# Forms of two pairs of inner channels made in one place, and a second new pass of each round begun by sums, in a gated-attention and MLP layer on one core

## The chip, the cores and the metric

The kernel runs on one core of one Trainium2 chip, launched once. The metric is the time on the device in microseconds; times given are the median of repeated runs. A profile is one more execution, recorded by the hardware profiler; its times count from the start of its span.

## What is computed

One layer (`DEPTH` is 1, so only the first mixer is used): RMSNorm, chunk-causal gated linear attention and its output projection, added to the residual; RMSNorm and an MLP with squared ReLU, added again; a last RMSNorm. 256 tokens, model width 2048, MLP width 8192, all in float32.

```python
def _sq_relu_mlp(h, w_up, w_down):
    a = jax.nn.relu(h @ w_up)
    return (a * a) @ w_down
...
    h = h + _gla_mixer(_rmsnorm(h, gla_norm[j]), ...)
    h = h + _sq_relu_mlp(_rmsnorm(h, mlp_norm[i]), mlp_w_up[i], mlp_w_down[i])
    return _rmsnorm(h, final_norm)
```

The change concerns the MLP. `w_up` is 2048 x 8192 and `w_down` 8192 x 2048.

## The kernel before

**Number format.** TensorE (PE) multiplies 128x128 stationary tiles by 256 moving columns. To keep float32 accuracy each operand is split in two parts, hi and lo: ScalarE (ACT) makes hi by a cast (L118) and VectorE (DVE) makes lo = raw - hi (L131, L154, L964). A product is three matmuls: hi by hi, hi by lo, lo by hi.

**Up.** `up()` (L701) works through 16 groups of 512 inner channels; each takes 8 up steps (L732), one for every two blocks of 128 rows of `w_up`, 24 matmuls a step, into two PSUM banks. When a group is complete, `ends` (L769) gives four pieces of work, one of which is issued behind each of the next four up steps (`piece`, L705): `normalized` (L785) applies ReLU and the RMSNorm scale on DVE, from PSUM into a tile of the pool tag t512; `forms` (L796) squares on ACT into `work[:, 2]` and makes sums and differences on DVE (L802); `form_parts` (L807) splits these into hi (ACT, L812) and lo (DVE, L813), which become stationary tiles of the down products.

**Down.** `down()` (L867) works in 8 rounds `m` of 1024 inner channels. A round is cut into 4 pairs `kp` of two blocks of 128 channels, and into up to four passes, one for each 512 output columns `g`. `order_of` (L667) runs the passes forwards and backwards in turn, so that the first pass of a round has the columns of the last pass of the round before. That one goes on in the same four PSUM banks; the other three passes are new ("fresh") and begin with copies between PSUM and SBUF on ACT (L828).

For one pair, the activations are a 2x2 block matrix (two halves of the tokens, two blocks of channels) and so is the weight. There are two ways to multiply them:

- by blocks: 8 products, 24 matmuls;
- by sums: 7 products of sums of blocks (the scheme of Strassen in Winograd's variant), 21 matmuls. DVE makes sums of the activations once for each pair (the forms S1 to S4) and sums of the weights for each pair and pass: three additions (L930, into `work[:, 0]` and `work[:, 1]` in turn). These sums are then cast (two casts of 512 columns, L118) and their lo is made (L964). In exchange the cast and lo of the weight itself need only 768 of 1024 columns.

`by_sums` (L671) says which way is taken:

```python
        if m == ROUNDS - 1:
            return (g, kp) in ((0, 2), (0, 3), (1, 2))
        if m == ROUNDS - 2 and g == order_of(m)[-1]:
            return kp == 1
        i = order_of(m).index(g)
        return kp > 0 or i == 1 or m > 0 and i == 0
```

A fresh pass whose first pair is by sums is `quick` (L886): two of its four banks are begun at the end of the pass before (L987) and the others while the first pair is at work (L911, L960).

**Order.** The driver (L1022) takes one up step with each pair of the down stage, 18 up steps ahead (`LEAD`, L681). PE's order is fixed by hand (`in_order`, L691). DVE and ACT are kept in order by `issue_after`: a lo follows the last weight sum, sums follow the lo, the copies of PSUM follow the last cast. What is left open is settled at build time by the framework's scheduler; each engine runs its own list in order. The weight slots `hi` and `lo` have five buffers each (L75), raw weights six (L135).

**Placement.** Up pairs listed in `even` (L718) have the second half of their weights shifted by 16 columns in the slot (L148) and, in the lo products, the halves in reverse order (L758).

**Other users of t512** (three buffers of 512 columns): the gate (L357), squares whose result is not used (L542, L619, L1033), `gate_out` (L558) and the diagonal tiles of `scale2_row` (L649).

Of the kernel before, what the change touches and what calls it, by code (L numbers as in the profile page):

```python
# [39 lines left out]
DV = 512  # L40
# [22 lines left out]
ROUNDS = HID // MR  # L63
# [5 lines left out]
def tile_gla_mlp(ctx, tc, x, xt, cols, w_vg, w_in, w_gate, w_out, w_up, w_down, final_norm, out):  # L69
    nc = tc.nc  # L70
# [5 lines left out]
    tmp = ctx.enter_context(tc.tile_pool(name="tmp", bufs=2))  # L76
# [232 lines left out]
    GR = 64 + RANK  # L309
# [44 lines left out]

    vh = big.tile([P, NT, D], F32R, tag="B", name="vh")
    vl = big.tile([P, NT, D], F32R, tag="B", name="vl")
    gn = tmp.tile([P, NT, GR], F32, tag="t512", name="gn", bufs=3)  # L357

    def put_v(bank, n, t, c0):
        nc.scalar.activation(vh[:, t, c0 : c0 + n], bank[:, :n], AF.Copy, scale=r1[:, t : t + 1])  # L360
# [5 lines left out]
    acc = natural(plain_x, rows(w_vg, 0, WMAX), WMAX, cuts, ahead=input_tile)  # L366
# [92 lines left out]
    for half in range(2):  # L459
        acc = turned(stream_x, w_in, KEYW + half * GT, even=(0,) if half else (2, 3), acc=None if half else [aux_bank(), aux_bank()])  # L460
# [18 lines left out]
    for half in range(2):  # L479
        acc = turned(stream_x, w_in, half * GT, even=())  # L480
# [41 lines left out]
    acc = natural(plain_x, rows(w_in, 3 * KEYW), G, HALF)  # L522
# [8 lines left out]
    def attend(hd, t):  # L531
        o = aux_bank()
        blocks = [(0, 0)] if t == 0 else [(0, P), (1, T)]
        vs = slice(hd * DV, (hd + 1) * DV)
        n = 0
        for src, lo in blocks:
            a_h, a_l = (a[hd][:, lo : lo + P] for a in (ath, atl))
            for s, v in ((a_h, vh), (a_h, vl), (a_l, vh)):
                halves(o, s, v[:, src, vs], n == 0, n == 3 * len(blocks) - 1)
                n += 1  # L540
        ss = st.tile([P, 1], F32, tag="oss", name="oss")
        sq = tmp.tile([P, DV], F32, tag="t512", name="sq", bufs=3)  # L542
        nc.scalar.activation(sq, o, AF.Square, scale=r1k[:, t : t + 1], accum_out=ss)
        nc.vector.tensor_scalar(ss, ss, 1.0 / DV, EPS, op0=ALU.mult, op1=ALU.add)
        rs = st.tile([P, 1], F32, tag="ors", name="ors")
        rsqrt(rs, ss)
        nc.vector.tensor_scalar(on[:, t, vs], o, r1k[:, t : t + 1], rs, op0=ALU.mult, op1=ALU.mult)
# [6 lines left out]
    def gate_out(acc, c0):  # L554
        for c in range(2):
            for t in range(NT):
                lo = c0 + 512 * c
                s = tmp.tile([P, 512], F32, tag="t512", name="sr", bufs=3)  # L558
                nc.scalar.activation(s, acc[t][c], AF.Silu, scale=r1[:, t : t + 1])
                nc.vector.tensor_tensor(on[:, t, lo : lo + 512], on[:, t, lo : lo + 512], s, op=ALU.mult)  # L560

# [14 lines left out]
    acc = natural(row_x, rows(w_in, 4 * KEYW), G, HALF, order=(EVEN[0], 0, EVEN[1], *(kt for kt in range(1, KT) if kt not in EVEN)))  # L576
# [24 lines left out]
    acc = natural(row_x, rows(w_in, 5 * KEYW), G, HALF)  # L601
# [13 lines left out]
    def ssq_h(c0):  # L615
        for t in range(NT):
            for c in range(2):
                lo = c0 + 512 * c
                sq = tmp.tile([P, 512], F32, tag="t512", name="sq", bufs=3)  # L619
                nc.scalar.activation(sq, h[:, t, lo : lo + 512], AF.Square, accum_out=hs[:, t, lo // 512 : lo // 512 + 1])  # L620

    acc = natural(row_o, rows(w_out, 0), G, HALF)
# [8 lines left out]
    acc = natural(row_o, rows(w_out, G), G, HALF)  # L631
# [13 lines left out]
    def scale2_row():  # L645

        b = aux_bank()
        for t in range(NT):
            d = tmp.tile([P, P], F32, tag="t512", name="diag", bufs=3)  # L649
            nc.vector.tensor_scalar(d, ident, r2[:, t : t + 1], None, op0=ALU.mult)  # L650
            nc.tensor.matmul(b[:, t * P : (t + 1) * P], ones, d, start=True, stop=True)
        nc.scalar.copy(r2row, b[:, :T])
# [3 lines left out]

    S3, S1, S2, S4, A12, A11, A22, A21 = range(8)
    KP = MR // P // 2  # L660
    GROUPS = D // GT
    work = mid.tile([P, 3 * G + T], F32, tag="qt", name="work")
    r2row = work[:, 3 * G :]
# [7 lines left out]
    def by_sums(m, g, kp):  # L671

        if m == ROUNDS - 1:
            return (g, kp) in ((0, 2), (0, 3), (1, 2))
        if m == ROUNDS - 2 and g == order_of(m)[-1]:
            return kp == 1
        i = order_of(m).index(g)
        return kp > 0 or i == 1 or m > 0 and i == 0


    LEAD = KT + 2  # L681
# [81 lines left out]
    def on_act(i):  # L763
        newest_form[0] = i.ins

    def on_vector(i):
        newest_form[1] = i.ins

    def ends(m, q, acc, taken):  # L769

        act = big.tile([P, 4 * G + 64], F32R, tag="BC"[q], name="act")[:, OFF:-16]
        acts[m][q] = act = act.rearrange("p (b i f s) -> p b i f s", b=2, i=2, f=8)
        normal = []

        def start():
            normal.extend(normalized(b) for b in acc)
            free.extend(taken)

        make = lambda b: forms(m, 2 * q + b, normal[b])
        split = lambda b: form_parts(m, 2 * q + b, act[:, b])  # L780
        if m == ROUNDS - 1 and q == MR // GT - 1:
            return [lambda: (start(), make(0)), lambda: split(0), lambda: make(1), lambda: split(1)]
        return [start, lambda: make(0), lambda: (split(0), make(1)), lambda: split(1)]

    def normalized(bank):  # L785
        s = tmp.tile([P, 2, T], F32, tag="t512", name="su", bufs=3)
        on_vector(nc.vector.scalar_tensor_tensor(
            s, bank.rearrange("p (i t) -> p i t", i=2), 0.0, r2row.unsqueeze(1).to_broadcast([P, 2, T]),
            op0=ALU.max, op1=ALU.mult,
        ))  # L790
        return s

    form = work[:, 2].rearrange("p (f s) -> p f s", f=8)
    ways_of = lambda m, kp: {by_sums(m, g, kp) for g in range(GROUPS)}

    def forms(m, kp, s):  # L796
        f = form
        on_act(nc.scalar.activation(
            f[:, A12:].rearrange("p (t i) s -> p i t s", t=2), s.rearrange("p i (t s) -> p i t s", t=2), AF.Square
        ))  # L800
        if True in ways_of(m, kp):
            sub = lambda o, x, y: on_vector(nc.vector.tensor_tensor(o, x, y, op=ALU.subtract))  # L802
            sub(f[:, S3 : S1 + 1], f[:, A21:].to_broadcast([P, 2, P]), f[:, A11 : A22 + 1])
            sub(f[:, S2], f[:, A11], f[:, S1])
            sub(f[:, S4], f[:, A12], f[:, S2])

    def form_parts(m, kp, act):  # L807
        ways = ways_of(m, kp)
        some = slice(0 if True in ways else A12, 8 if False in ways else A21)
        x = form[:, some].rearrange("p f s -> p (f s)")  # L810
        oh, ol = (act[:, i, some].rearrange("p f s -> p (f s)") for i in range(2))
        on_act(nc.scalar.copy(oh, x))  # L812
        on_vector(nc.vector.tensor_tensor(ol, x, oh.bitcast(F32), op=ALU.subtract))  # L813

    def stationary(m, kp, f):
        return [acts[m][kp // 2][:, kp % 2, i, f] for i in range(2)]
# [3 lines left out]
    n_sums = [0]  # L820
# [46 lines left out]
    def down(passes):  # L867
# [7 lines left out]
        for n, (m, g) in enumerate(passes):  # L875
# [11 lines left out]
            for kp in range(KP):  # L887
# [35 lines left out]
                block = lambda i, n=1: slice(i * T, (i + n) * T)  # L923
                if by_parts:
                    these = (P16, 0, at(A11), block(1)), (B32, T, at(A12), block(3)), (B32, 0, at(S4), block(2))
                    wk = work[:, n_sums[0] % 2]
                    n_sums[0] += 1
                    u = wk.rearrange("p (f s) -> p f s", f=4)
                    raw = raw.rearrange("p (f s) -> p f s", f=4)
                    add = lambda o, x, y: nc.vector.tensor_tensor(o, x, y, op=ALU.add)  # L930

                    with tc.issue_after(last_lo[0].ins):
                        add(u[:, :2], raw[:, :1].to_broadcast([P, 2, T]), raw[:, 1:3])
                        add(u[:, 2], u[:, 0], raw[:, 2])
                        last_sum[0] = add(u[:, 3], u[:, 2], raw[:, 3]).ins
                else:
                    these = [
                        (k, 0, at(f[i]), block(2 * i, 2))
                        for i in range(2) for k, f in ((B32, (A11, A12)), (BX4, (A21, A22)))
                    ]  # L940
# [89 lines left out]

    def square(t, src):
        n = src.shape[-1]
        sq = tmp.tile([P, 512], F32, tag="t512", name="sqf", bufs=3)  # L1033
# [15 lines left out]

    def last_step(kt, w, t, c):  # L1050
        lo, hi = cuts[t][c]
        a = stationary(ROUNDS - 1, kt // 2, (A11, A21)[t] - kt % 2)
# [94 lines left out]
```

## Time and profile before

| | |
|---|---|
| median of 3 runs | 1056.26 us (1055.80 to 1056.47) |
| profiled execution | 1056.75 us |
| its span in the profile | 1054.7 us |
| granted TensorE clock | 0.999 |
| matmuls | 9136 |
| read from and written to HBM | 206.92 MB and 2.10 MB |

The difference between the profiled execution and its span lies before the first and behind the last recorded instruction. A row of instructions shows line, engine, operation, tiles (written <- read), their size and number; in the view by time it shows the start, the length, and in brackets the idle time of the engine before it with what ended it. Lengths of neighbouring instructions overlap, since the next begins before the last results of one are written; the pace of an engine is read from start to start. In the view of stretches each engine has its busy time and, in brackets, its number of instructions.

### The profile page before, as it was taken

The numbers are of one execution on the slowest core, as the hardware profiler recorded it, in microseconds if no ns is written. First come the engines' busy times: TensorE is split into PE (matmuls) and PEld (weight loads), VectorE is DVE, ScalarE is ACT, GpSimd is POOL, SyncE is SP. The second block draws the span as 40 slices with busy tenths as digits, with TensorE's granted clock in tenths as the row PEclk, the third lists the DMA queues.
The fourth block names the chain that finished last, engine by engine and source line by source line (L and its number), as shares of the span: only waits on it lengthen the run. The fifth ranks groups of instructions, "written<-read, shape, count | busy, mean of one in ns | idle before, by whom it ended". The sixth has DMA issues, their size and how long they took to land.

```text
span 1054.7 us, 22398 instructions
## 1 busy us (share of the span) xinstructions
PE 1045.4 (99%) x9136; PEld 1044.4 (99%) x9136; DVE 844.4 (80%) x1169; ACT 697.5 (66%) x1017; POOL 12.7 (1%) x39
## 2 busy tenths in 40 slices
PE   9999999999999999999999999999999999999997
PEld 8999999999999999999999999999999999999997
DVE  5768645656465566889999999999999999999887
ACT  5785544546455455677678778777777777777685
POOL 0000000010000000000000000000000000000000
PEclk9999999999999999999999999999999999999999
DMA  9857665556656666567566566666666666666673
GB/s 341 314 177 212 192 197 160 160 147 177 197 180 181 186 194 180 158 193 226 172 209 217 193 208 207 199 202 201 216 200 202 220 200 201 202 199 207 213 214 127
DMA packets 94790, 210.46 MB, mean 200 GB/s; under 512 B 6704, under 2 KB 7344, under 8 KB 94560
## 3 DMA queue, kind: packets, MB, share of 16 engines
q1 hardware_dynamic: 94016, 207.38, 63.0%
q10 hardware_dynamic: 672, 1.66, 0.5%
q8 instruction: 71, 1.16, 0.5%
q14 instruction: 31, 0.25, 0.1%
HBM read 206.92 MB, written 2.10 MB: 198 GB/s over the span
## 4 chain that ended last, share of the span: by engine, by line
PE 96%; DMA 2%; issue 0%; ACT 0%; SPq 0%; DVE 0%; POOLq 0%; POOL 0%; DVEq 0%; ACTq 0%
PE up L699 33%; PE acc L699 28%; PE acc L165 25%; PE acc L205 6%; PE aux L205 2%; DMA raw<-in_w_vg 1%; PE aux L165 1%; PE aux L568 1%; DMA zz<-in_xt 1%; PE aux L496 1%; SPq L157 0%; ACT sqf L1034 0%; DVE lo L131 0%; ACT hi L118 0%; PE acc L397 0%
## 5 line engine op out<-in xcount | busy, mean ns | idle before, releaser
L118 ACT CAST hi<-raw 128x1024 fp32r<-128x1024 f32 (+3 forms) x386 | 372.7, 986 | 169.8 <-PE acc L165 106.2
L131 DVE TENSOR_TENSOR lo<-raw,hi 128x1024 fp32r<-128x1024 f32 (+3 forms) x226 | 245.7, 1089 | 117.2 <-ACT hi L118 115.7
L699 PE MATMUL acc<-hi,act 128*128 128x256 f32 x1724 | 247.0, 276 | 0.0
L699 PE MATMUL up<-hl,hi 128*128 128x256 f32 x1024 | 239.4, 276 | 0.0
L699 PE MATMUL up<-hh,hi 128*128 128x256 f32 x1024 | 239.3, 276 | 0.0
L154 DVE TENSOR_TENSOR lo<-raw,hi 128x1024 fp32r<-128x1024 f32 x160 | 194.9, 1220 | 36.8 <-ACT hi L118 34.5
L699 PEld LDWEIGHTS acc<-hi,act 128*128 128x128 f32 x1724 | 219.2, 188 | 0.0
L118 ACT CAST hi<-work 128x512 fp32r<-128x512 f32 x196 | 119.9, 622 | 119.0 <-DVE work L930 108.3
L699 PEld LDWEIGHTS up<-hl,hi 128*128 128x128 f32 x1024 | 192.3, 188 | 0.0
L699 PEld LDWEIGHTS up<-hh,hi 128*128 128x128 f32 x1024 | 192.3, 188 | 0.0
L699 PE MATMUL up<-hh,lo 128*128 128x256 f32 x1024 | 137.4, 276 | 0.0
L699 PE MATMUL acc<-lo,act 128*128 128x256 f32 x862 | 134.1, 276 | 0.0
L964 DVE TENSOR_TENSOR lo<-work,hi 128x1024 fp32r<-128x1024 f32 x98 | 119.5, 1220 | 8.9 <-ACT hi L118 8.9
L699 PEld LDWEIGHTS up<-hh,lo 128*128 128x128 f32 x1024 | 126.0, 188 | 0.0
L699 PEld LDWEIGHTS acc<-lo,act 128*128 128x128 f32 x862 | 114.4, 188 | 0.0
L165 PE MATMUL acc<-hi,xA 128*128 128x256 f32 (+1 forms) x736 | 104.7, 279 | 1.0 <-ACT hi L118 1.0
L165 PEld LDWEIGHTS acc<-hi,xA 128*128 128x128 f32 x736 | 93.7, 188 | 1.7 <-ACT hi L118 1.7
L930 DVE TENSOR_TENSOR work<-work,raw 128x256 f32<-128x256 f32 x196 | 83.1, 424 | 5.1
L930 DVE TENSOR_TENSOR work<-raw 128x512 f32<-128x512 f32 x98 | 67.1, 685 | 0.0
L165 PE MATMUL acc<-lo,xA 128*128 128x256 f32 (+1 forms) x368 | 58.5, 278 | 0.1
L165 PEld LDWEIGHTS acc<-lo,xA 128*128 128x128 f32 x368 | 49.6, 188 | 0.3 <-DVE lo L131 0.3
L205 PE MATMUL acc<-xA,hi 128*128 128x256 f32 x288 | 49.2, 276 | 0.0
(158 smaller groups left out, 1148.4 us busy)
## 6 DMA issues: line engine op xcount, KB each, us to landing
raw<-in_w_up SPq DMA_DIRECT2D x128, 512.0 KB, 4.7
raw<-in_w_down SPq DMA_DIRECT2D x128, 512.0 KB, 4.1
raw<-in_w_in SPq DMA_DIRECT2D x80, 512.0 KB, 3.8
raw<-in_w_out SPq DMA_DIRECT2D x32, 512.0 KB, 3.7
raw<-in_w_vg SPq DMA_DIRECT2D x14, 520.0 KB, 8.6
h<-in_x SPq DMA_DIRECT2D x4, 512.0 KB, 8.9
out<-hf SPq DMA_DIRECT2D x5, 256.0 KB, 2.6
zz<-in_xt SPq DMA_DIRECT2D x3, 384.0 KB, 8.2
```

The costliest lines, as they stand in the source:

```text
L118: last_hi[0] = nc.scalar.copy(to, raw)
L131: last_lo[0] = nc.vector.tensor_tensor(lo[:, s], raw[:, s], hi[:, s].bitcast(F32), op=ALU.subtract)
L154: last_lo[0] = nc.vector.tensor_tensor(to[1], dst, to[0].bitcast(F32), op=ALU.subtract)
L165: nc.tensor.matmul(o[:, m], x, w[:, m], start=first and c == 0, stop=last, skip_group_check=True)
L205: nc.tensor.matmul(o, u[:, i, s], m, start=kt == 0 and n == 0 and j % 2 == 0, stop=kt == KT - 1 and n == 2, skip_group_check=True,)
L496: nc.tensor.matmul(o, kab[:, k[0], c0 + c, k[1] : k[1] + P], q(qt[:, c0 + c]), start=c == 0, stop=c == 1)
L568: nc.tensor.transpose(b[:, o + t * P : o + (t + 1) * P], src[:, t, kt * P : (kt + 1) * P], ident)
L699: newest[0] = nc.tensor.matmul(o, x, w, start=first, stop=last, skip_group_check=True).ins
L930: add = lambda o, x, y: nc.vector.tensor_tensor(o, x, y, op=ALU.add)
L964: last_lo[0] = nc.vector.tensor_tensor(to[1][:, :G], wk, to[0][:, :G].bitcast(F32), op=ALU.subtract)
```

## The change

1. `by_sums` takes the first pair of pass i = 3 by sums, as well as that of i = 1 (in rounds 0 to 5).
2. `forms` works for both pairs of a group at once, in `work[:, 1:]` (2048 columns, where one pair had `work[:, 2]`). `normalized` writes there; one square in place of two, three subtractions twice as wide in place of six. The pieces of a group become: both ReLUs; the forms of both pairs; the split of the first; the split of the second. The last group has three pieces in place of four.
3. The weight sums use `work[:, 0]` and a new tile `spare` (2 x 512 columns) in turn. `spare` takes the room of two of the three t512 buffers; it also serves `gate_out` (three of the four tiles) and the diagonal tiles.
4. The forms are renumbered, so that the block that was second is stored in order of PSUM.

```diff
-    gn = tmp.tile([P, NT, GR], F32, tag="t512", name="gn", bufs=3)
+    gn = tmp.tile([P, NT, GR], F32, tag="t512", name="gn", bufs=1)
+    spare = tmp.tile([P, 2, 512], F32, tag="spare", name="spare", bufs=1)
...
-                s = tmp.tile([P, 512], F32, tag="t512", name="sr", bufs=3)
+                i = 2 * c + t
+                s = tmp.tile([P, 512], F32, tag="t512", name="sr", bufs=1) if i % 3 == 2 else spare[:, i % 3]
...
-            d = tmp.tile([P, P], F32, tag="t512", name="diag", bufs=3)
+            d = spare[:, t, :P]
...
-    S3, S1, S2, S4, A12, A11, A22, A21 = range(8)
+    S1, S3, S2, S4, A12, A22, A11, A21 = range(8)
...
-        return kp > 0 or i == 1 or m > 0 and i == 0
+        return kp > 0 or i in (1, 3) or m > 0 and i == 0
...
+    form = work[:, 1:].rearrange("p b (f s) -> p b f s", f=8)
     def ends(m, q, acc, taken):
-        normal = []
         def start():
-            normal.extend(normalized(b) for b in acc)
+            for b in range(2):
+                normalized(acc[b], form[:, b, A12:])
             free.extend(taken)
-        make = lambda b: forms(m, 2 * q + b, normal[b])
-        split = lambda b: form_parts(m, 2 * q + b, act[:, b])
+        split = lambda b: form_parts(m, 2 * q + b, form[:, b], act[:, b])
         if m == ROUNDS - 1 and q == MR // GT - 1:
-            return [lambda: (start(), make(0)), lambda: split(0), lambda: make(1), lambda: split(1)]
-        return [start, lambda: make(0), lambda: (split(0), make(1)), lambda: split(1)]
+            return [lambda: (start(), forms(m, q)), lambda: split(0), lambda: split(1)]
+        return [start, lambda: forms(m, q), lambda: split(0), lambda: split(1)]
...
-    def forms(m, kp, s):
-        on_act(nc.scalar.activation(
-            f[:, A12:].rearrange("p (t i) s -> p i t s", t=2), s.rearrange("p i (t s) -> p i t s", t=2), AF.Square
-        ))
-        if True in ways_of(m, kp):
-            sub(f[:, S3 : S1 + 1], f[:, A21:].to_broadcast([P, 2, P]), f[:, A11 : A22 + 1])
-            sub(f[:, S2], f[:, A11], f[:, S1])
-            sub(f[:, S4], f[:, A12], f[:, S2])
+    def forms(m, q):
+        on_act(nc.scalar.activation(f[:, :, A12:], f[:, :, A12:], AF.Square))
+        if any(True in ways_of(m, 2 * q + b) for b in range(2)):
+            sub(f[:, :, S1 : S3 + 1], f[:, :, A21:].to_broadcast([P, 2, 2, P]), f[:, :, A22 : A11 + 1])
+            sub(f[:, :, S2], f[:, :, A11], f[:, :, S1])
+            sub(f[:, :, S4], f[:, :, A12], f[:, :, S2])
...
-                    wk = work[:, n_sums[0] % 2]
+                    wk = work[:, 0] if n_sums[0] % 2 else spare.rearrange("p b c -> p (b c)")
```

More of the change, by code (lines that the diff above doesn't have):

```diff
@@ L541, in attend @@
         ss = st.tile([P, 1], F32, tag="oss", name="oss")
-        sq = tmp.tile([P, DV], F32, tag="t512", name="sq", bufs=3)
+        sq = tmp.tile([P, DV], F32, tag="t512", name="sq", bufs=1)
         nc.scalar.activation(sq, o, AF.Square, scale=r1k[:, t : t + 1], accum_out=ss)
@@ L618, in ssq_h @@
                 lo = c0 + 512 * c
-                sq = tmp.tile([P, 512], F32, tag="t512", name="sq", bufs=3)
+                sq = tmp.tile([P, 512], F32, tag="t512", name="sq", bufs=1)
                 nc.scalar.activation(sq, h[:, t, lo : lo + 512], AF.Square, accum_out=hs[:, t, lo // 512 : lo // 512 + 1])
@@ L783, in ends, with normalized @@
-        return [start, lambda: make(0), lambda: (split(0), make(1)), lambda: split(1)]
-    def normalized(bank):
-        s = tmp.tile([P, 2, T], F32, tag="t512", name="su", bufs=3)
+            return [lambda: (start(), forms(m, q)), lambda: split(0), lambda: split(1)]
+        return [start, lambda: forms(m, q), lambda: split(0), lambda: split(1)]
+    def normalized(bank, to):
         on_vector(nc.vector.scalar_tensor_tensor(
-            s, bank.rearrange("p (i t) -> p i t", i=2), 0.0, r2row.unsqueeze(1).to_broadcast([P, 2, T]),
-            op0=ALU.max, op1=ALU.mult,
-        ))
-        return s
@@ L793, in tile_gla_mlp @@
-    form = work[:, 2].rearrange("p (f s) -> p f s", f=8)
+            to.rearrange("p (i t) s -> p i (t s)", i=2), bank.rearrange("p (i t) -> p i t", i=2), 0.0,
+            r2row.unsqueeze(1).to_broadcast([P, 2, T]), op0=ALU.max, op1=ALU.mult,
+        ))
     ways_of = lambda m, kp: {by_sums(m, g, kp) for g in range(GROUPS)}
-    def forms(m, kp, s):
+    def forms(m, q):
         f = form
-        on_act(nc.scalar.activation(
-            f[:, A12:].rearrange("p (t i) s -> p i t s", t=2), s.rearrange("p i (t s) -> p i t s", t=2), AF.Square
-        ))
-        if True in ways_of(m, kp):
+        on_act(nc.scalar.activation(f[:, :, A12:], f[:, :, A12:], AF.Square))
+        if any(True in ways_of(m, 2 * q + b) for b in range(2)):
@@ L802, in forms @@
             sub = lambda o, x, y: on_vector(nc.vector.tensor_tensor(o, x, y, op=ALU.subtract))
-            sub(f[:, S3 : S1 + 1], f[:, A21:].to_broadcast([P, 2, P]), f[:, A11 : A22 + 1])
-            sub(f[:, S2], f[:, A11], f[:, S1])
-            sub(f[:, S4], f[:, A12], f[:, S2])
-    def form_parts(m, kp, act):
+            sub(f[:, :, S1 : S3 + 1], f[:, :, A21:].to_broadcast([P, 2, 2, P]), f[:, :, A22 : A11 + 1])
+            sub(f[:, :, S2], f[:, :, A11], f[:, :, S1])
+            sub(f[:, :, S4], f[:, :, A12], f[:, :, S2])
@@ L808, in form_parts @@
+    def form_parts(m, kp, f, act):
         ways = ways_of(m, kp)
         some = slice(0 if True in ways else A12, 8 if False in ways else A21)
-        x = form[:, some].rearrange("p f s -> p (f s)")
+        x = f[:, some].rearrange("p f s -> p (f s)")
         oh, ol = (act[:, i, some].rearrange("p f s -> p (f s)") for i in range(2))
@@ L1032, in square @@
         n = src.shape[-1]
-        sq = tmp.tile([P, 512], F32, tag="t512", name="sqf", bufs=3)
+        sq = tmp.tile([P, 512], F32, tag="t512", name="sqf", bufs=1)
         nc.scalar.activation(sq[:, :n], src, AF.Square, accum_out=fs[:, t, n_fs[t] : n_fs[t] + 1])
@@ L1051, in last_step @@
         lo, hi = cuts[t][c]
-        a = stationary(ROUNDS - 1, kt // 2, (A11, A21)[t] - kt % 2)
+        a = stationary(ROUNDS - 1, kt // 2, ((A11, A12), (A21, A22))[t][kt % 2])
         for i, (x, y) in enumerate(((0, 0), (0, 1), (1, 0))):
```

## Prediction

> **What bounds the kernel now.** I read the head of the page, then TensorE (PE) by stretches, the chain, and VectorE (DVE) and ScalarE (ACT) instruction by instruction through one round. Numbers in the rows of time are us: start, length, what.
>
> ```profile
> span 1054.7 us, 22398 instructions
> PE 1045.4 (99%) x9136; PEld 1044.4 (99%) x9136; DVE 844.4 (80%) x1169; ACT 697.5 (66%) x1017; POOL 12.7 (1%) x39
> ```
>
> PE never rests, so only matmuls taken away, or waits added, can move the end. The average of 80% for DVE hides the stage that matters. Here is one round of the MLP by stretches (busy time and instructions of PE, PEld, DVE, ACT, POOL):
>
> ```profile
> 672.80:693.40 20.60, 20.60 (x184) 20.60 (x184) 20.50 (x32) 14.56 (x20) 0.00 (x0) 1.00 0.55 173
> 693.40:714.00 20.60, 20.60 (x184) 20.60 (x183) 19.84 (x27) 15.78 (x24) 0.00 (x0) 1.00 0.69 222
> 714.00:734.50 20.50, 20.50 (x184) 20.50 (x183) 19.81 (x29) 17.33 (x26) 0.00 (x0) 1.00 0.61 192
> 734.50:755.10 20.60, 20.60 (x184) 20.60 (x183) 18.35 (x24) 14.92 (x22) 0.00 (x0) 1.00 0.73 233
> ```
>
> DVE is busy 78.5 of 82.3 us: PE binds, with DVE 4.6% behind. I call a pair of inner channels of one down pass, with the up step beside it, a unit; a round has 16, u0 to u15, four to each pass. A unit by sums has 21 + 24 = 45 matmuls, one by blocks (a light unit) 24 + 24 = 48. Today u8 and u12 are light in rounds 1 to 5.
>
> The chain in one round, PE's pieces with their matmuls:
>
> ```profile
> 715.26 1.93 PE acc L699 x17
> 720.36 3.63 PE acc L699 x32
> 741.10 3.63 PE acc L699 x32
> ```
>
> A matmul takes 3.63 / 32 = 0.1134. The x32 pieces are the last 8 of the unit before and the 24 of a light unit, so u8 starts at 721.27 and u12 at 742.0. u7 starts at 715.26 + 8 x 0.1134 = 716.17. A heavy unit is 5.10 us, a light one 5.44, so u13 starts at 747.45; a round is 82.3.
>
> **What the change takes away.** `by_sums` now also holds for the first pair of the last pass (i = 3) in rounds 0 to 5 (round 6 returns earlier, in round 7 nothing changes): six light units u12 become heavy. 6 x 3 = 18 matmuls x 0.1134 = **2.04 us** less on PE. The compiled order of the changed kernel has 9087 matmuls in place of 9105; the DMA queue of SP and the work of POOL are in the same order.
>
> **What it adds to DVE.** A heavy unit, and the light u8 with the start of u9, on DVE:
>
> ```profile
> 703.03 0.96 DVE L131 TENSOR_TENSOR lo<-raw,hi 128x768 fp32r<-128x768 f32 x1 [0.29 <-ACT hi L118]
> 703.90 0.69 DVE L930 TENSOR_TENSOR work<-raw 128x512 f32<-128x512 f32 x1
> 704.62 0.88 DVE L930 TENSOR_TENSOR work<-work,raw 128x256 f32<-128x256 f32 x2
> 705.43 1.22 DVE L154 TENSOR_TENSOR lo<-raw,hi 128x1024 fp32r<-128x1024 f32 x1
> ...
> 707.70 0.95 DVE L131 TENSOR_TENSOR lo<-raw,hi 128x768 fp32r<-128x768 f32 x1
> 718.55 1.22 DVE L131 TENSOR_TENSOR lo<-raw,hi 128x1024 fp32r<-128x1024 f32 x1
> 719.69 0.61 DVE L802 TENSOR_TENSOR work<-work 128x128 f32<-128x128 f32 x2
> 720.22 1.22 DVE L154 TENSOR_TENSOR lo<-raw,hi 128x1024 fp32r<-128x1024 f32 x1
> 721.35 0.95 DVE L131 TENSOR_TENSOR lo<-raw,hi 128x768 fp32r<-128x768 f32 x1
> ```
>
> Instructions overlap, so I count from start to start. The heavy unit takes 707.70 - 703.03 = 4.67. The light one takes (719.69 - 718.55) + (721.35 - 720.22) = 2.27 without the two forms. Each new heavy unit costs DVE 2.4 us.
>
> **What the merged forms give back.** Today each pair has one subtraction 256 wide and two 128 wide; after it one 512 and two 256 wide serve two pairs.
>
> ```profile
> 683.22 0.69 DVE L930 TENSOR_TENSOR work<-raw 128x512 f32<-128x512 f32 x1
> 683.83 0.42 DVE L802 TENSOR_TENSOR work<-work 128x256 f32<-128x256 f32 x1
> 684.16 0.42 DVE L930 TENSOR_TENSOR work<-work,raw 128x256 f32<-128x256 f32 x1
> 684.50 0.29 DVE L802 TENSOR_TENSOR work<-work 128x128 f32<-128x128 f32 x1
> 684.70 0.42 DVE L930 TENSOR_TENSOR work<-work,raw 128x256 f32<-128x256 f32 x1
> ```
>
> Start to start: 512 wide 0.61, 256 wide 0.33, 128 wide 0.20. Before 2 x (0.33 + 0.20 + 0.20) = 1.46, after 0.61 + 0.33 + 0.33 = 1.27: 0.2 saved for each up group of 512 channels, 0.4 a round. The square becomes one instruction 1024 wide; a cast that wide starts 0.95 after its predecessor (rows below), two of 512 take 1.06: 0.1 of ACT.
>
> [...]
>
> Sum for DVE in a round: 78.5 busy, about 0.5 lost between dependent additions (in each unit by sums 704.59 to 704.62, and as much inside the pair), + 2.4 - 0.4 = 81.0. PE: 15 x 5.10 + 5.44 = 82.0. DVE alone still fits, by 1.0 us.
>
> **What ACT takes of that 1.0.** A pass that begins by sums has two accumulator copies each ahead of two of its casts. Pass i = 1 (u4, u5) does so today:
>
> ```profile
> 695.55 0.63 ACT L118 CAST hi<-work 128x512 fp32r<-128x512 f32 x1 [0.22 <-DVE work L930]
> 696.09 0.58 ACT L828 COPY acc<-h 128x512 f32<-128x512 f32 x1
> ...
> 697.12 0.83 ACT L118 CAST hi<-raw 128x768 fp32r<-128x768 f32 x1
> 697.99 0.96 DVE L131 TENSOR_TENSOR lo<-raw,hi 128x768 fp32r<-128x768 f32 x1 [0.19 <-ACT hi L118]
> ```
>
> The cast is done 2.4 after the last addition, DVE would be there after 2.27. So DVE loses 0.28 at u4 (693.05, the row below, to 697.99 is 4.94, not 4.66) and 0.38 at u5 (697.99 to 703.03): 0.66 per pass. This wait is tied to DVE's own additions, not to PE. In the changed kernel u12 and u13 have the same ACT order, so two passes lose 1.32.
>
> A third loss is new. From the square before u8 to the cast of u10, ACT runs almost without a gap; the DVE rows are the additions before that square, an idle stretch and the start of u10:
>
> ```profile
> 716.59 0.63 ACT L798 ACTIVATE work<-su 128x512 f32<-128x512 f32 x1
> 717.12 1.04 ACT L118 CAST hi<-raw 128x1024 fp32r<-128x1024 f32 x1
> 718.07 1.10 ACT L828 COPY acc<-h 128x512 f32<-128x512 f32 x2
> 721.19 0.59 ACT L828 COPY sums<-acc 128x512 f32<-128x512 f32 x1 [0.30 <-PE acc L699]
> 727.61 1.80 ACT L118 CAST hi<-raw 128x768 fp32r<-128x768 f32 x2
> 715.14 0.89 DVE L930 TENSOR_TENSOR work<-work,raw 128x256 f32<-128x256 f32 x2
> 726.79 1.23 DVE L964 TENSOR_TENSOR lo<-work,hi 128x1024 fp32r<-128x1024 f32 x1 [0.48 <-ACT hi L118]
> 728.50 0.96 DVE L131 TENSOR_TENSOR lo<-raw,hi 128x768 fp32r<-128x768 f32 x1
> ```
>
> ACT: from 716.59 to 727.61 are 11.0, less the 0.30 for PE 10.7. In the changed order the first square is 0.42 longer, the second (0.53) is gone, and the cast of the second pair's form (0.84 by start to start), which today stands in u10, comes ahead of u10's cast: 11.45. With one cast of the sums before the square (0.56) and u10's own (0.83), 12.85 from the additions' end. DVE: 728.50 - 716.03 = 12.47, of which 0.48 idle; with the wider forms (0.27 before u8, 0.24 in it) 12.5. DVE loses about 0.4 there. So 1.32 + 0.4 = 1.7 lost against 1.0 spare: **0.7 us a round short**. PE must then wait that much in a round, once the store is used up.
>
> **The store.** How far DVE is ahead:
>
> ```profile
> 693.05 0.95 DVE L131 TENSOR_TENSOR lo<-raw,hi 128x768 fp32r<-128x768 f32 x1
> 713.55 0.95 DVE L131 TENSOR_TENSOR lo<-raw,hi 128x768 fp32r<-128x768 f32 x1
> 741.29 0.95 DVE L131 TENSOR_TENSOR lo<-raw,hi 128x768 fp32r<-128x768 f32 x1
> ```
>
> In u7 the part is ready at 714.50 and wanted after six matmuls, at 716.85: 2.35 ahead. In u13, behind the light u12, 742.24 against 748.13: 5.9. That refill goes. By the same steps u10 starts on DVE 2.9 ahead of PE in round 1 (the copy that waits for PE at 721.19 sets it), u2 of the next round 1.5 ahead, where 0.4 is needed; each later round is 0.7 lower. Three further rounds end in stalls: about 0.5 + 0.75 + 0.75 = 2.0.
>
> A stall costs more than itself. Matmuls in 20 us, at full clock (column PEclk):
>
> ```profile
> 30.00:50.00 20.00, 20.00 (x169) 20.00 (x168) 14.50 (x19) 15.02 (x21) 1.07 (x2) 1.00 0.87 302
> 210.00:230.00 20.00, 20.00 (x179) 20.00 (x178) 11.34 (x16) 8.86 (x15) 2.75 (x5) 1.00 0.48 140
> ```
>
> With two or three in each count that lie across an edge, PE's pace is some 5% slower in the first: 0.2 us a unit. I read it as left behind by a wait, until the shifted pair of `even` (L718, in u4) comes by. From u2 to u4 that is 0.4 in a round, and it gives DVE time, so it largely replaces a later stall. I add 0.4 in all.
>
> **Sum.** -2.04 + 2.0 + 0.4 = +0.4 us on the profiled 1056.75 (span 1054.7 and 2.05 around it), 0.5 above the median of 1056.26: 1056.7 against the median.
>
> Costed at nothing: `normalized` writes the same width elsewhere; squares into one t512 buffer follow each other on ACT alone; `gate_out` keeps three buffers; the sums keep two (work and `spare`); the last group has three pieces for four, where PE has no wait. If a form's subtraction waits for the wider square, 0.4 at most a group, 0.8 a round, falls on DVE.
>
> **Rivals.** (a) *The cover holds*: the copies of u12 are absorbed, DVE keeps 1.0 spare, no stall: 1056.26 - 2.04 = 1054.2. For it: DVE loses as much at u4 and u5 today and PE never waits. Against: no second refill. [...]
> (b) *Slower*: PE waits behind u4, in u5 to u15, and keeps the slow pace until the next u4. It decides once u7 or u8 is under 0.4 ahead. Ten units x 0.2 = 2 us a round, in three rounds 6, with 0.7 for the first stalls: 1056.26 - 2.04 + 6.7 = 1061. Against: my ledger has u2 as the lowest point.
> (c) *It doesn't do what it says*: PE's order shows 18 fewer matmuls; under 1%.
>
> **How the numbers follow.** Forecast, 1055 to 1058.4: 0.50; (a) 0.27; (b) 0.22. A run tells 0.2%, 2.1 us, from no change, so the bounds are 1054.15 and 1058.37. (a) lies on the first: 0.10 of it faster, 0.17 same. (b) is slower, with 0.03 of the forecast. Faster 0.10, same 0.65, slower 0.25. An error of 0.3 us a round in the ledger moves the end by 1.4; the range is 1054.1 to 1060.0.
>
> **What would show it.** Right: 18 matmuls fewer; DVE at 98% and more of rounds 2 to 5; waits of PE for DVE or ACT in u1 to u4 from round 3 on, absent before; DVE idle 0.2 to 0.4 at u12 and u13. Wrong: no wait of PE and rounds of 82.0 us (then (a)); matmuls at 0.118 through most of a round (then (b)); a form waiting for its square.

## The result, and the profile after

| | before | after |
|---|---|---|
| median | 1056.37 us (1055.80 to 1056.60) | 1061.91 us (1061.53 to 1061.93) |
| profiled execution | 1056.75 us | 1061.93 us |
| its span | 1054.7 us | 1060.0 us |
| granted TensorE clock | 0.999 | 0.999 |
| matmuls | 9136 | 9118 |

The ratio is 1.0052 (95% interval 1.0035 to 1.0070): 0.5% or 5.5 us longer, clear of the noise, and above the predicted range (1054.1 to 1060.0). The head of the page after:

```profile
span 1060.0 us, 22328 instructions
PE 1050.6 (99%) x9118; PEld 1048.9 (99%) x9118; DVE 855.6 (81%) x1148; ACT 701.4 (66%) x1013; POOL 11.7 (1%) x39
```

The 18 matmuls are gone and PE is still busy 99%, for 5.2 us longer. So a matmul must have become slower, or waits must be hidden in "busy". To see where, I read four points of time from each trace (us):

| kernel | first up product | last up product | last matmul ends | end of span |
|---|---|---|---|---|
| before | 380.95 | 998.44 | 1047.57 | 1054.71 |
| after | 380.54 | 1001.05 | 1052.09 | 1060.02 |

From the first to the last up product: 617.49 before, 620.51 after, 3.0 more where 18 matmuls fewer should have given 2.0 less, so 5.1 lost. From there to the last matmul, where the work is the same: 49.13 and 51.04, 1.9 lost. From the last matmul to the end: 7.14 and 7.93, 0.8 lost. Against it stands an MLP that happened to begin 0.4 earlier. -2.04 + 5.1 + 1.9 + 0.8 - 0.4 = 5.4; the spans differ by 5.3.

**PE's waits.** What PE waited for between 430 and 1040 us, in the view of waits (us in total, times, longest); before has no such line:

```profile
PEld acc L702 <- DVE lo L131: 0.9, 4, 0.4
...
PE acc L702 <- DVE lo L131: 0.2, 1, 0.2
PEld acc L702 <- DVE lo L964: 0.2, 1, 0.2
```

These three lines make 1.3 us in all. One of the waits by time, in round 3, u2 (start, length, operation, number):

```profile
689.53 0.84 PE L702 MATMUL acc<-hi,act 128*128 128x256 f32 x6
690.35 0.62 PE L702 MATMUL acc<-lo,act 128*128 128x256 f32 x3
...
691.04 0.28 PE L702 MATMUL up<-hh,hi 128*128 128x256 f32 x1
...
692.22 0.28 PE L702 MATMUL up<-hh,hi 128*128 128x256 f32 x1
```

Six matmuls from 689.53 should end in a start at 690.21; the next starts at 690.35, and one more is late behind it. From then on ten matmuls take 692.22 - 691.04 = 1.18: 0.118 each, not 0.1134. Starts later than they should be lie at 607.7, 690.2, 772.8, 855.6, 938.3 and 968.7: rounds 2 to 6 in u2, and a last one at the border of u7 and u8 of round 6.

Not every late start changes the pace. The longest, in round 6, does not:

```profile
938.81 0.61 PE L702 MATMUL acc<-lo,act 128*128 128x256 f32 x3 [0.23 <-DVE lo L131]
939.26 0.28 PE L702 MATMUL up<-hh,hi 128*128 128x256 f32 x1
...
941.53 0.68 PE L702 MATMUL up<-hh,lo 128*128 128x256 f32 x4
```

Six matmuls from 937.74 and these three should end in a start at 938.76; it comes at 939.26, 0.50 late. But the next 20 take 941.53 - 939.26 = 2.27: 0.1134 each. Only a second late start there, of 0.05 in the products at 941.53, is followed by 0.118.

**The pace.** Equal stretches, one between two waits (behind the shifted pair), one near the end (columns: PE, PEld, DVE, ACT, POOL, each busy time and number; then granted clock, share of DMA, GB/s):

```profile
710.00:750.00 40.00, 40.00 (x355) 40.00 (x355) 38.72 (x51) 33.11 (x49) 0.00 (x0) 1.00 0.66 207
...
1000.00:1040.00 40.00, 40.00 (x342) 40.00 (x341) 33.72 (x44) 31.52 (x47) 0.00 (x0) 1.00 0.59 186
```

13 matmuls fewer in 40 us, with PE counted as busy throughout and the clock granted in full in both. The busy share can't show this; the count in a stretch does.

### The profile page after: what moved, and what is told of

It is laid out like the page before. It is cut to its first block, busy times and chain, and to the rows that moved or that the text cites. A ratio compares the mean times of both kernels' runs of the same rounds, so it can differ in the third digit from the quotient of the medians.

```text
span 1060.0 us, 22328 instructions
## 1 busy us (share of the span) xinstructions
PE 1050.6 (99%) x9118; PEld 1048.9 (99%) x9118; DVE 855.6 (81%) x1148; ACT 701.4 (66%) x1013; POOL 11.7 (1%) x39
## 4 chain that ended last, share of the span: by engine, by line
PE 94%; DVE 2%; DMA 2%; issue 1%; SPq 0%; ACT 0%; POOLq 0%; POOL 0%; DVEq 0%; ACTq 0%
PE up L702 32%; PE acc L702 27%; PE acc L165 25%; PE acc L205 6%; PE aux L205 2%; DMA raw<-in_w_vg 1%; PE aux L165 1%; DMA zz<-in_xt 1%; PE aux L571 1%; PE aux L498 1%; DVE lo L131 0%; DVE lo L154 0%; DVE lo L964 0%; DVE act L813 0%; DVE spare L930 0%
## 5 line engine op out<-in xcount | busy, mean ns | idle before, releaser
L702 PE MATMUL acc<-hi,act 128*128 128x256 f32 x1712 | 249.6, 277 | 0.0
L118 ACT CAST hi<-spare 128x512 fp32r<-128x512 f32 x104 | 63.9, 621 | 65.8 <-DVE spare L930 52.9
L118 ACT CAST hi<-work 128x512 fp32r<-128x512 f32 x104 | 63.7, 622 | 64.5 <-DVE work L930 43.0
L964 DVE TENSOR_TENSOR lo<-work,hi 128x1024 fp32r<-128x1024 f32 x52 | 63.3, 1218 | 1.0 <-ACT hi L118 1.0
L964 DVE TENSOR_TENSOR lo<-spare,hi 128x1024 fp32r<-128x1024 f32 x52 | 63.3, 1218 | 0.1
```

What stands on the lines that cost most here:

```text
L118: last_hi[0] = nc.scalar.copy(to, raw)
L702: newest[0] = nc.tensor.matmul(o, x, w, start=first, stop=last, skip_group_check=True).ins
L964: last_lo[0] = nc.vector.tensor_tensor(to[1][:, :G], wk, to[0][:, :G].bitcast(F32), op=ALU.subtract)
```

## Experiments

Each expectation sets theory **W** against a rival of its own. W: DVE's round is longer than PE's, so PE waits once DVE's lead (the store) is used up, and a wait leaves PE at 0.118 until a shifted pair of `even` comes. The rivals put the loss elsewhere: in a slow pace that comes or goes by itself (R, D), in the merged forms and their places (P), in the new pass as such, with its copies on ACT (Q). In the expectations e1 is the run of the merged forms alone, e2 of the sums alone, e5 of the kernel before without the shifted pair. Ratios are to the kernel before, run beside each.

### The shifted pair left out, in both kernels

```diff
-        even = ((6,), (0,))[q] if m == 0 else (6,) if q == 0 else ()
+        even = ((6,), (0,))[q] if m == 0 else ()
```

In the kernel after:

> The changed kernel with the shifted up pair in round 0 alone (no shifted pair in rounds 1 to 7). Theory W with the reading that a wait leaves PE in a pace of 0.118 until a shifted pair comes by: the first wait (round 2, u2, at about 608 us) is followed by the slow pace to the end, 442 us at 4.1% = 18 us, in place of the 5.9 us of slow pace now; DVE gains 0.2 us a unit on PE, so the later waits (1.4 us) go, and 0.5 for the shifted pairs: 1072, between 1069 and 1075. Rival R (the slow pace ends by itself, or is caused by what DVE and ACT do at the time): 1061 to 1063.

In the kernel before:

> The kernel before, with the shifted up pair in round 0 alone. Theory W: PE never waits there after 399 us, so nothing has to be undone; the seven shifted pairs cost 12 matmuls of 0.12 in place of 0.113 us each, 0.55 in all: 1055.8, between 1055.5 and 1056.4. Rival D (the pace falls off by itself, without a wait, and the shifted pair is what keeps it up): up to 590 us at 4.1%, 1060 to 1080.

Measured: the kernel after without it 1072.17 us, ratio 1.0152 (1.0136 to 1.0167); the kernel before without it 1055.85 us, 0.9998 (0.9989 to 1.0007). Stretches of the kernel after without it, the first of them ahead of its only wait (607.9):

```profile
560.00:600.00 40.00, 40.00 (x356) 40.00 (x355) 38.75 (x53) 30.68 (x47) 0.00 (x0) 1.00 0.60 199
620.00:660.00 40.00, 40.00 (x342) 40.00 (x341) 38.72 (x52) 32.52 (x49) 0.00 (x0) 1.00 0.65 211
...
1000.00:1040.00 40.00, 40.00 (x342) 40.00 (x341) 30.88 (x40) 28.08 (x42) 0.00 (x0) 1.00 0.61 198
```

One wait, and PE keeps the lower pace for 450 us. It never waits again, since DVE, no faster than before, now has time. 1056.0 (the kernel before beside it) + 454 us x (1 - 0.1134 / 0.118) = 17.7, less 2.0 for the matmuls, with 0.8 at the end: 1072.5. So W's reading of the pace holds here, and R falls: the pace doesn't end by itself. D falls by the kernel before, where the pace stays whole without the shifted pair (355 or 356 matmuls in each of four stretches of 40 us between 560 and 1040); where PE never waits, that pair changes nothing that the times show.

### A shifted pair later, in the last round

```diff
-        even = ((6,), (0,))[q] if m == 0 else (6,) if q == 0 else ()
+        even = ((6,), (0,))[q] if m == 0 else (6,) if q == 0 else (4,) if m == ROUNDS - 1 else ()
```

> The changed kernel with one more shifted up pair, the fifth of the last up group, which falls in u10 of round 6, some 10 us behind the wait at 969 us. Theory W (the wait there leaves PE slow to the end): the slow pace ends at about 981 us, 69 us x 4.1% = 2.9 less; but PE at full pace meets the wait of the last round that the run with the merged forms alone showed at 1013 us (0.25 and some 35 us of slow pace, 1.4), so 1061.9 - 2.9 + 1.6 = 1060.6, between 1058.9 and 1061.2, with matmuls at 0.113 from 981 to about 1015. Rival R (the tail is slow for a reason of its own): slow to the end, 1061.9.

Measured: 1061.23 us, ratio 1.0045 (1.0030 to 1.0060).

```profile
970.00:983.00 13.00, 13.00 (x113) 13.00 (x112) 12.62 (x19) 11.86 (x19) 0.00 (x0) 1.00 0.63 198
986.00:1012.00 26.00, 26.00 (x232) 26.00 (x231) 22.80 (x29) 18.41 (x25) 0.00 (x0) 1.00 0.57 185
1017.00:1040.00 23.00, 23.00 (x198) 23.00 (x197) 19.90 (x26) 19.74 (x32) 0.00 (x0) 1.00 0.61 207
```

By one microsecond: 8.69, 8.92, 8.61 matmuls. The pace comes back with the added pair at 984, which shows what the pair does, and is lost again at 1015, by a wait that the kernel after hides under its low pace. That one has its own cause (next). The time is 0.7 under that of the kernel after, where 1.3 was expected (it lies 0.03 above the expected range), and the two intervals overlap; the counts of matmuls show the pair's effect, the times don't.

### The merged forms alone

The kernel after, with the pass i = 3 as it was:

```diff
-        return kp > 0 or i in (1, 3) or m > 0 and i == 0
+        return kp > 0 or i == 1 or m > 0 and i == 0
```

> The merged forms, the tile spare and the renumbering stay; the first pair of pass i = 3 goes back to blocks, so 18 matmuls come back. Theory W (the loss is PE waiting for DVE, once the store ahead of PE is used up, and PE's slower pace after each wait): DVE has its second refill again and 0.4 us a round to spare, no wait in the MLP, pace 0.1133 us a matmul throughout: 1056.4, between 1055.9 and 1056.8. Rival P (the new places of forms and sums, or the wider instructions, slow PE): most of the loss stays, 1060 to 1064.

Measured: 1058.47 us, ratio 1.0019 (1.0010 to 1.0029); in the profile no wait of PE in rounds 0 to 6 and one in the last, at 1013.5. That is neither W's 1056.4 nor P's 1060 to 1064. (Its ten runs lie between 1056.68 and 1059.12; the profile is of the longest.) The waits there (1000 to 1020 us), and PE at that place:

```profile
ACT work L800 <- DVE work L791: 3.9, 1, 3.9
...
DVE work L802 <- ACT work L800: 1.1, 1, 1.1
...
PEld acc L702 <- DVE lo L964: 0.2, 1, 0.2
```

```profile
1012.69 1.07 PE L702 MATMUL acc<-hi,act 128*128 128x256 f32 x8
1013.73 0.74 PE L702 MATMUL acc<-lo,act 128*128 128x256 f32 x4
```

Eight matmuls from 1012.69 should end at 1013.60. The last group has three pieces; the first holds ReLUs, square and subtractions in one, so DVE stands 1.1 at L802 until the wider square is done, and the lo behind it is late by some tenths.

### The last group in four pieces again

The same, with the special case in `ends` taken out:

```diff
-        if m == ROUNDS - 1 and q == MR // GT - 1:
-            return [lambda: (start(), forms(m, q)), lambda: split(0), lambda: split(1)]
```

> The merged forms alone (as in e1), with the last group in four pieces like every other. Theory L (the wait at 1013 us in e1 comes from the last group's ReLUs, square and forms in one piece: DVE waited 1.1 us there for the square, ACT 3.9 for the ReLUs): the wait and the slow pace of the last 35 us go, 1058.5 falls to 1056.3, between 1055.9 and 1056.7. Rival S (the wait comes from the sums that alternate between work and spare): 1058.5 stays.

Measured: 1056.96 us, ratio 1.0007 (0.9997 to 1.0016), and no wait of PE in the MLP. The three pieces were the cause of the wait at 1013.5. The pace is normal (28 matmuls from 1012.46 to 1015.64: 0.1136 each), but from the last matmul to the end of the span are still 7.73, where before has 7.14.

### The last squares in three places

The same, with the squares of the last norm (L1034) in the t512 buffer and the two halves of `spare` in turn:

```diff
-        sq = tmp.tile([P, 512], F32, tag="t512", name="sqf", bufs=1)
+        k = sum(n_fs) % 3
+        sq = tmp.tile([P, 512], F32, tag="t512", name="sqf", bufs=1) if k == 2 else spare[:, k]
```

> The merged forms with the last group in four pieces (1056.96 us against 1056.24 of its runs of the kernel before), and the last squares (sqf) written to three places in turn, the t512 buffer and the two halves of spare, as the kernel before has three buffers. Theory T (the one buffer holds the squares apart on ACT, and the first half of the tokens is stored later): a square begins 0.10 us after the read of the accumulator before it, not 0.21 to 0.23; from the last matmul to the end 7.15 us, not 7.7; 1056.4 us, within 0.1% of the kernel before. Rival (the end is late for another reason, such as the stores themselves): the squares follow directly, but the end is still 7.6 to 7.9 us behind the last matmul, 1056.9 us.

Measured: 1056.46 us, ratio 1.0001 (0.9992 to 1.0010). ACT at the first squares, in one buffer and, behind it, in three places:

```profile
1042.80 0.19 ACT L1032 ACTIVATION_READ_ACCUMULATOR sqf<-h 128x1 f32 x1
1043.03 0.63 ACT L1032 ACTIVATE sqf<-h 128x512 f32<-128x512 f32 x1
```

```profile
1042.53 0.19 ACT L1033 ACTIVATION_READ_ACCUMULATOR spare<-h 128x1 f32 x1
1042.62 0.62 ACT L1033 ACTIVATE spare<-h 128x512 f32<-128x512 f32 x1
```

0.23 from the start of the read of the accumulator to the next square, against 0.09. The last norm of the first half of the tokens is late by it, and its first store too. SP's queue in the two:

```profile
1046.21 4.68 SPq L1105 DMA_DIRECT2D out<-hf  x8
```

```profile
1045.20 5.29 SPq L1106 DMA_DIRECT2D out<-hf  x8
```

From the last matmul to the end: 7.73 and 7.13 (1047.65 to 1055.38; 1047.37 to 1054.50). So 0.6 at the end is the price of one buffer. The two medians differ by 0.5 and their intervals overlap, so the times alone don't show it; the traces do: this end takes 7.58 to 7.93 in the five with one buffer, and 7.13 to 7.31 in the nine with three places.

### The sums alone

The kernel before, with the pass i = 3 by sums:

```diff
-        return kp > 0 or i == 1 or m > 0 and i == 0
+        return kp > 0 or i in (1, 3) or m > 0 and i == 0
```

> The kernel before with the first pair of pass i = 3 by sums, forms made pair by pair as before. Theory W: DVE has 0.4 us a round more to do than in the changed kernel (ledger 83.1 against 82.7 us a round), so PE waits earlier and more: 1061.9 + 4 to 5 rounds of 0.4 = 1063.7, between 1062.5 and 1065.5, with waits in u1 to u4 and a slow tail. Rival P: the forms and sums are in their old places, so the 18 matmuls are simply gone: 1054.4.

Measured: 1060.94 us, ratio 1.0047 (1.0032 to 1.0062), 2.8 us less than expected and below the expected range. Its rounds on DVE (start of u7's lo to the next) take 82.60 to 82.73, those of the kernel after 82.74: on balance the merged forms take nothing off DVE's round, and I had expected more without them. PE waits at 692.2, 700.7, 774.8, 857.6, 940.4 and 968.2: from round 3 on, one round later than after. The first of them leaves the pace whole, the others don't: 8.9 matmuls a microsecond from 712 to 750 (338), 8.6 behind the last wait, from 970 to 990 (172), and 8.7 from 692.5 to 709 (143), with the wait at 700.7 in between. Here it is mostly the lo of the up step that is late:

```profile
PEld up L699 <- DVE lo L154: 1.5, 4, 0.5
```

### The sums without the work of the forms

The same, with the subtractions of `forms` (L802) left out in rounds 1 to 6 (so the sums work with stale forms):

```diff
-        if True in ways_of(m, kp):
+        if True in ways_of(m, kp) and m in (0, ROUNDS - 1):
```

> The kernel before with the first pair of pass i = 3 by sums (as in e2) and without the sums and differences of the forms (L802) in rounds 1 to 6: that part of the computation is left out. DVE has 2 x 1.46 = 2.9 us a round less to do. Theory W (DVE's round of 82.7 us against PE's 82.0 is what makes PE wait): DVE's round falls to 79.8, no wait in rounds 2 to 6, no slow pace, all 18 matmuls gained: 1056.0 - 2.0 = 1054.0, between 1053.5 and 1054.6. Rival Q (the quick pass as such, with its bank copies on ACT, makes PE wait): waits stay, 1057 to 1061.

Measured: 1054.33 us, ratio 0.9980 (0.9971 to 0.9990), and no wait of PE. With 1.46 us less on DVE for each two pairs (start to start, as in the prediction), the 18 matmuls give the 1.9 that they should. DVE's work is what turns the gain into a loss, and rival Q falls: the new pass and its copies are all there.

### The sums in some of the rounds

```diff
-        return kp > 0 or i == 1 or m > 0 and i == 0
+        return kp > 0 or i == 1 or i == 3 and m in (0, 1, 3, 5) or m > 0 and i == 0
```

> The kernel before with the first pair of pass i = 3 by sums in rounds 0, 1, 3 and 5 alone. Theory W (each such round takes some 0.7 us from a store that an ordinary round refills): the store lasts for two rounds from the start and for one round later, no wait up to round 5; 4 x 0.34 = 1.36 gained: 1054.7. If the sums of round 6 on DVE meet a low store, one wait near 968 us and a slow tail add 3.6: 1058.3. Rival Q (each quick pass makes its own wait): 4 waits with slow pace to u4, 1057 or more.

Measured: 1058.61 us, ratio 1.0021 (1.0011 to 1.0031), one wait:

```profile
965.94 0.62 PE L699 MATMUL acc<-hi,act 128*128 128x256 f32 x4
966.62 0.74 PE L699 MATMUL acc<-lo,act 128*128 128x256 f32 x4
```

The second should start at 966.39: the same place, at the border of u7 and u8 of round 6, as the last wait in the kernel after. With rounds 0, 1 and 3 alone:

> The kernel before with the first pair of pass i = 3 by sums in rounds 0, 1 and 3 alone, so that rounds 4 and 5 refill the store ahead of the extra sums of round 6. Theory W: no wait anywhere in the MLP, 3 x 3 matmuls = 1.02 us gained: 1055.2 beside 1056.2, between 1054.9 and 1055.7. Rival Q (the quick pass costs by itself): no gain or a loss, 1056.2 and more.

Measured: 1055.25 us, ratio 0.9991 (0.9982 to 1.0000), no wait. Nine matmuls fewer are 1.0; 0.9 was measured. Three more matmuls saved in round 5 cost 3.4 (1058.61 against 1055.25). Some 0.3 of waiting and 83 us at 0.118, the pace of the kernel after behind the same place (342 matmuls in 40 us), come to 3.5.

The same without the shifted pair behind round 0 (the edit of the first experiment):

> The same with the shifted up pair in round 0 alone. Theory W: with no wait to undo, the seven shifted pairs are a cost: 0.55 less by their matmuls, 0.2 by what e5 showed: 1054.8, between 1054.3 and 1055.3. If a run meets a wait, it keeps the slow pace to the end and lies several us higher.

Measured: 1054.97 us, ratio 0.9988 (0.9979 to 0.9997). It is the fastest version that leaves nothing out, 1.2 us under before, and rests on PE never waiting (355 or 356 matmuls in each of four stretches of 40 us between 560 and 1040).

### The same with the merged forms

To that version I added the merged forms, with the last group in four pieces and the squares in three places:

> The same, with the first pair of pass i = 3 by sums in rounds 0, 1 and 3 and the shifted pair in round 0 alone: the fastest version so far (1054.97 us, with the forms of before) with the merged forms. If the merged forms only change how far DVE is ahead, and PE waits in neither, the time is the same: 1055.0 us, no wait of PE in the MLP. If they are worth something of their own, 0.4 us a round or 2.8 in all, 1052.2. If the later work of ACT at u8 to u10 takes the rest of the store, there is one wait of PE behind 960, followed by a slow pace to the end: 1058.5.

Measured: 1072.25 us, ratio 1.0148 (1.0132 to 1.0163): none of the three. DVE at u2 of round 2 with merged forms, then without:

```profile
605.89 1.09 DVE L811 TENSOR_TENSOR act<-work,act 128x896 fp32r<-128x896 f32 x1
606.90 0.95 DVE L131 TENSOR_TENSOR lo<-raw,hi 128x768 fp32r<-128x768 f32 x1
...
609.29 1.22 DVE L154 TENSOR_TENSOR lo<-raw,hi 128x1024 fp32r<-128x1024 f32 x1
```

```profile
605.76 0.96 DVE L131 TENSOR_TENSOR lo<-raw,hi 128x768 fp32r<-128x768 f32 x1
...
607.24 1.09 DVE L813 TENSOR_TENSOR act<-work,act 128x896 fp32r<-128x896 f32 x1
...
609.04 1.22 DVE L154 TENSOR_TENSOR lo<-raw,hi 128x1024 fp32r<-128x1024 f32 x1
```

With merged forms the second pair's forms are ready one unit earlier, so their split (L811, L813 in the other) goes ahead of u2's weight lo, not behind it: that lo starts 1.14 later, at the point where the store is lowest. The same order stands in the kernel after (split at 605.60, lo at 606.60; in the kernel before lo at 605.14, split at 606.61). Here PE waits for it:

```profile
607.18 0.84 PE L702 MATMUL acc<-hi,act 128*128 128x256 f32 x6
607.90 0.61 PE L702 MATMUL acc<-lo,act 128*128 128x256 f32 x3
608.35 0.28 PE L702 MATMUL up<-hh,hi 128*128 128x256 f32 x1
```

Nine matmuls from 607.18 should end in a start at 608.20; it comes at 608.35, 0.15 late. The pace stays whole: 15 matmuls from there to 610.05 take 0.1133 each. The up step's lo is 0.25 later, ready at 610.51. The weight loads there:

```profile
610.05 0.53 PEld L702 LDWEIGHTS acc<-hi,act 128*128 128x128 f32 x4
610.56 1.00 PEld L702 LDWEIGHTS up<-hh,lo 128*128 128x128 f32 x8
```

Four loads at 0.1134 put the next one at 610.51; it starts at 610.56, 0.05 late. The eight matmuls of this product take 1.15, where those of the unit before took 1.07:

```profile
605.37 1.07 PE L702 MATMUL up<-hh,lo 128*128 128x256 f32 x8
...
610.62 1.15 PE L702 MATMUL up<-hh,lo 128*128 128x256 f32 x8
```

And so the lower pace stays to the end, though this delay is the shorter of the two. In 40 us:

```profile
560.00:600.00 40.00, 40.00 (x355) 40.00 (x354) 38.76 (x53) 30.69 (x46) 0.00 (x0) 1.00 0.60 197
620.00:660.00 40.00, 40.00 (x342) 40.00 (x341) 38.77 (x50) 31.49 (x46) 0.00 (x0) 1.00 0.68 213
```

## Why the prediction was wrong, step by step

**Right: matmuls and DVE's round.** 18 fewer; without waits they are worth the forecast 2.04 (1.9 in the run without the work of the forms). DVE's round, start of u7's lo to the next:

```profile
631.77 0.95 DVE L131 TENSOR_TENSOR lo<-raw,hi 128x768 fp32r<-128x768 f32 x1
...
714.51 0.95 DVE L131 TENSOR_TENSOR lo<-raw,hi 128x768 fp32r<-128x768 f32 x1
```

82.74, where the ledger gave 81.0 + 1.7 = 82.7 against PE's 82.0. Its three losses to ACT are there too (idle time in brackets), at u10, u12 and u13:

```profile
729.90 0.96 DVE L131 TENSOR_TENSOR lo<-raw,hi 128x768 fp32r<-128x768 f32 x1 [0.32 <-ACT hi L118]
739.50 0.96 DVE L131 TENSOR_TENSOR lo<-raw,hi 128x768 fp32r<-128x768 f32 x1 [0.19 <-ACT hi L118]
744.55 0.96 DVE L131 TENSOR_TENSOR lo<-raw,hi 128x768 fp32r<-128x768 f32 x1 [0.29 <-ACT hi L118]
```

So rival (a) was rightly set aside: its cover didn't hold. One term was too large, the 0.4 that the merged forms give back. Without them the round is 82.60 to 82.73, and the idle 0.32 at u10 stands in the merged order alone, so by this difference they give back about 0.2.

**Wrong: "Three further rounds end in stalls".** Five did, rounds 2 to 6. Up to 968 the lost time is 5.1 less what belongs to the last wait (0.3, and 32 us at 0.118, or 1.3): 3.5, which is 0.7 a round, as forecast, but five times, where I had 2.0. What failed is the start of the count, "u2 of the next round 1.5 ahead": I took DVE's order at u2 from before, where the second pair's split stands behind the lo. The change moves it ahead, and the lo starts 1.14 us later, which takes the 1.5 down to the 0.4 that is needed. The runs with sums in rounds 0, 1 and 3, with merged forms and without, show it. That is one of the two rounds too many: the sums alone, with DVE's old order, wait in u2 of four rounds, 3 to 6, not three. Which figure of the count is one round short is not shown. I had read the new order for ACT at u8 to u10, and not for DVE at the place that I myself called the lowest.

**Wrong in size: "I add 0.4 in all".** From a wait in u2 to the shifted pair in u4 are about 120 matmuls x 0.0046 = 0.55. That it "largely replaces a later stall" holds: in a round like the third 0.25 of waiting and 0.55 of pace together are close to the 0.74 by which DVE's round is longer than PE's. It needs no further 0.4; it is the form in which most of the stall is paid.

**Wrong by omission: round 6, and what follows it.** The ledger was one of rounds 2 to 5. In round 6 DVE has additions of the last sums besides (L1006, L1010), some 1.3 us from u6 to u8:

```profile
960.63 0.42 DVE L1006 TENSOR_TENSOR sums<-sums 128x256 f32<-128x256 f32 x1
...
964.17 0.41 DVE L1006 TENSOR_TENSOR sums<-sums 128x256 f32<-128x256 f32 x1
...
967.16 0.68 DVE L1010 TENSOR_TENSOR h<-h,sums 128x512 f32<-128x512 f32 x1
967.76 1.22 DVE L964 TENSOR_TENSOR lo<-spare,hi 128x1024 fp32r<-128x1024 f32 x1
```

That lo is ready at 968.98 (967.76 + 1.22); PE wants it at 968.85, four matmuls from 968.40. Before, with the same additions, it was ready at 966.92 and wanted at 967.73:

```profile
965.70 1.22 DVE L964 TENSOR_TENSOR lo<-work,hi 128x1024 fp32r<-128x1024 f32 x1
...
967.73 0.62 PE L699 MATMUL acc<-lo,act 128*128 128x256 f32 x4
```

Without the additions it would be ready some 1.3 earlier, in time; no run leaves them out, but with DVE's lead refilled by ordinary rounds 4 and 5 the wait is gone (1055.25). Since no shifted pair comes behind this wait, the pace stays at 0.118 for the last 83 us: 0.3 + 3.2 = 3.5, more than half of the slowdown. This is rival (b)'s mechanism (a wait behind u4 that keeps the slow pace), and its total of 1061 was close, but for the wrong reason: I priced it for three rounds between 2 and 5, with ten units each, and it came once, at the end, where nothing resets it.

**Wrong: "Costed at nothing".** Squares into one t512 buffer do follow each other on ACT alone, but 0.14 later each, and the last norm has nothing to cover it: 0.6 (0.8 in the kernel after). The last group's three pieces: alone they make a wait (1058.47, gone with four pieces); in the kernel after the pace was low by then, and no wait shows.

Sum with measured sizes: -2.04 + 3.5 + 3.5 + 0.8 = 5.8, which is what the points of time give without the earlier start.

**Open.** Why a late weight load leaves PE at 0.118, why some do not, and why a shifted pair ends it, no run tells. In all kept traces I count 26 late starts behind 430 us; 22 are followed by 0.118 and four are not (0.15 to 0.50 late), so how late it is does not decide. All 15 slow stretches there that met a shifted pair ended in it, and none ended otherwise. The granted clock does not explain the pace: in the kernel after it is 1.00 both from 710 to 750 us (355 matmuls in 40 us) and from 1000 to 1040 (342).

## What to carry to other kernels

Where PE is busy all the time, count its matmuls in equal stretches: "99% busy" hid a pace 4% lower here (0.118 us a matmul, not 0.1134). Price a wait by what follows it, up to the next event that restores the pace, and look first at the last one, behind which nothing does (here 0.3 us of waiting and 3.2 of low pace). When the partner engine's margin is tenths of a microsecond, read the new order of its instructions at the point of lowest margin, and do the ledger again for the first and last rounds, whose work differs.

## What the runs showed of the hardware

- After 22 of 26 late starts of PE, matmuls of 256 columns with a new weight tile each ran at 0.118 us, not 0.1134, at the same granted clock, for 450 us where nothing intervened. A weight load 0.05 late was enough, in the version that took 1072.25 us, 3 us behind one 0.15 late that left the pace whole; the version without merged forms, where neither was late, took 1054.97.
- Weight tiles shifted by 16 columns (64 bytes) in the slot, with the halves in reverse order, ended this, 15 times of 15; which of the two does it was not tried. Where PE never waits, leaving them out changed nothing that the times show (ratio 0.9998).
- A square on ACT that writes the buffer of the square before started 0.23 after the start of the read of the accumulator, one that writes elsewhere 0.09.
